# Two transformer blocks on one core: the same instructions, other SBUF addresses

## The chip, the core and the metric

The kernel runs on one core of a Trainium2 chip. The metric is the device time of one execution in microseconds (us), as the median of several runs. The profile comes from one further execution, taken by the hardware profiler; its engines are PE (TensorE, the matmuls), PEld (TensorE's weight loads, which run beside PE), DVE (VectorE), ACT (ScalarE), POOL (GpSimd) and SP (which issues most DMAs).

## What is computed

A network of two blocks of two layers each, for 256 tokens of `x` and 256 tokens of context, all in float32 with a model width of 1024. Cut to its skeleton:

```python
def first_block(x, c, ctx, ...):
    for i in range(2):
        sh1, sc1, ga1, sh2, sc2, ga2 = split(silu(c) @ w_ada[i] + b_ada[i], 6)
        hx = rms_norm(x, g_mix[i]) * (1 + sc1) + sh1
        zx = hx @ w_in[i]
        mx = concat([attention(q, k, v), pool_mix(...), fourier_mix(...)])
        x = x + ga1 * (mx @ w_out[i])
        fx = rms_norm(x, g_ffn[i]) * (1 + sc2) + sh2
        x = x + ga2 * swiglu(fx, w_gate_up[i], w_down[i])
        ...
def second_block(x, c, ctx, ...):
    for i in range(2):
        ...
        y = merge_branches(conv, differential_attention, gates)
        x = x + gx1 * y
        x = x + gx2 * (square(relu(h @ w1)) @ w2)
def reference(...):
    return second_block(first_block(x, ...), ...)
```

The context stream goes through the same steps, except in the last layer of each block. Most of the work is the product of 256 or 512 token columns with large weight matrices.

## The kernel before

**The product.** Activations lie in SBUF feature by feature: 128 features on the partitions, 256 or 512 tokens along each partition. So that a product in the fast `float32r` format keeps float32 accuracy, both operands are split into a high and a low half, and three products are summed in PSUM: high times high, high times low, low times high. Weights come in pieces of 512 rows by 256 columns: `load` (L89) issues one DMA into a `raw` tile of 128 x 1024, `wunits` (L97) makes the high half `wh` with a cast on ACT (L110) and the low half `wl` with a subtraction on DVE, or in some stages on POOL (L111). The pools `raw`, `whp` and `wlp` hold 3, 4 and 4 such tiles.

**Which operand moves.** In `proj` (L120) the weight slice is the stationary operand of 128 x 128 and the activation is the moving one, 512 or 256 columns wide. These are L142 (high, high), L143 (high, low) and L144 (low, high). L165 to L167 in `proj_split` and L528 to L530 in `proj_early` are the same with 256 columns. In `projt` (L170), which makes queries, keys, values and other token-major results, it is the other way round: the activation is stationary and the weight slice moves, 256 columns, in L184 to L186. `shift_product` (L487) has a stationary operand of only four columns per chunk, `sh[:, k, :]`, and moves the weight slices past it (L493). Two lines of `proj` and one of `shift_product`:

```python
nc.tensor.matmul(o, lhsT=hi[k][:, w], rhs=a, start=(k == order[0]), stop=False)   # L142
nc.tensor.matmul(o, lhsT=hi[k][:, w], rhs=b, start=False, stop=False)             # L143
nc.tensor.matmul(ps[:4, :256], lhsT=sh[:, k, :], rhs=w[k], ...)                   # L493
```

**Other places that the text speaks of.** Attention keeps its probabilities and their transposes in the pool `ap`: L663 writes an exponential into a fresh `ap` tile, L673 transposes it on PE, L867 copies the transpose into another, and L846 reads that in the product with the values. The convolution of the second block (`tap`, L1040) runs on DVE in L1060: for each of 31 taps it multiplies the input, shifted by d = -15 to 15 tokens, by a weight and adds it into an accumulator tile; with both streams its shape is 2 x (256 - |d|) elements, so 128x500 is a shift of 6 tokens, 24 bytes. The modulation vectors are made by `ada_load` and `ada_mul` (L311) from weights that are loaded straight into `act` tiles.

**What sets the order.** Source order, priorities (`soon`, `first`) and the tile scheduler. Each engine then works through its own list of instructions in order.

**Where the tiles lie.** Pools are placed one behind the other in the order in which `Net.__init__` makes them. In the built program (bytes per partition) the constants start at 16512 and hold some small tiles, then `raw` follows at 34016, `whp` at 46304, `wlp` at 62688, `act` at 89632. So every `raw`, `wh` and `wl` tile starts 96 bytes past a multiple of 128, and every tile of `act`, `tmp`, `ap`, `hd`, `zo` and `po` 32 bytes past one. Slices step by 512 or 1024 bytes and keep that remainder. Every float32r product thus has its moving and its stationary operand at the same place modulo 64 bytes, namely 32, save the 64 of L493.

Of the kernel before, what the change touches and what calls it, by code (L numbers as in the profile page):

```python
# [12 lines left out]
F32R = mybir.dt.float32r  # L13
# [5 lines left out]
P = 128  # L19
D = 1024  # L20
KC = 8
T = 256
EPS = 1e-6
NACT = 42
# [3 lines left out]
class Net:  # L28
    def __init__(self, ctx, tc, a, out):
        self.tc, self.nc, self.a, self.out = tc, tc.nc, a, out  # L30
        pool = lambda name, bufs, **k: ctx.enter_context(tc.tile_pool(name=name, bufs=bufs, **k))
        self.cp = pool("cp", 1)
        self.raw = pool("raw", 3)
        self.whp = pool("whp", 4)
        self.wlp = pool("wlp", 4)
        self.lay = pool("lay", 2)
        self.pools = {
            "act": (pool("act", NACT), 512),
            "tmp": (pool("tmp", 5), 512),
            "ap": (pool("ap", 11), 512),  # L40
            "hd": (pool("hd", 4), 512),
            "zo": (pool("zo", 3), 512),
            "po": (pool("po", 4), 256),
            "ti": (pool("ti", 6), 16),
            "tn": (pool("tn", 4), 16),
            "th": (pool("th", 8), 16),
            "ta": (pool("ta", 20), 16),
        }
        self.psum = {n: pool("ps" + n, b, space=PSUM) for n, b in
                     (("mm", 3), ("S", 2), ("T", 1), ("po", 1), ("ms", 1))}  # L50
        self.n = 0
        self.queue = []
        self.bg = []
        self.loaded, self.summed = [], []
        self.lo_count, self.lo_share = 0, 0
        self.depth = 2
        self.count, self.rate, self.held, self.gap = 0, 1, False, False
        self.units = []
        self.late = []
# [37 lines left out]
    def wunits(self, src):  # L97

        nc = self.nc
        kk = src.shape[0] // P  # L100
        hi, lo = [], []
        k = 0
        while k < kk:
            m = min(4, kk - k)
            with self.soon():
                raw = self.load(src[k * P : (k + m) * P, :])
                h = self.whp.tile([P, 1024], F32R, tag="wh", name=self.nm("wh"))
                l = self.wlp.tile([P, 1024], F32R, tag="wl", name=self.nm("wl"))
                r = raw[:, : m * 256]
                nc.scalar.copy(h[:, : m * 256], r)  # L110
                self.lo_engine().tensor_tensor(l[:, : m * 256], r, h[:, : m * 256].bitcast(F32), op=ALU.subtract)  # L111
            for i in range(m):
                hi.append(h[:, i * 256 : (i + 1) * 256])
                lo.append(l[:, i * 256 : (i + 1) * 256])
            k += m
        if not self.held:
            self.tick()
        return hi, lo
# [107 lines left out]

    def setup(self):
        nc = self.nc
        self.ident = self.const([P, P], "ident")
        make_identity(nc, self.ident)  # L230
        self.ones = self.const([P, 1], "ones")
        nc.vector.memset(self.ones, 1.0)
        self.lnw = self.const([P, P], "lnw")
        nc.vector.memset(self.lnw, 1.0 / 512)
        self.mhalf = self.const([P, 16], "mhalf")
        nc.vector.memset(self.mhalf, -0.5)
        self.xT = [self.const([P, 512], f"xT{k}") for k in range(KC)]
        self.cv = {}

    def cond(self, sfx):  # L240
# [1158 lines left out]
```

## Time and profile before

| | us |
|---|---|
| median of 3 runs (2423.03 to 2424.59) | 2423.99 |
| the profiled execution, its own time | 2417.76 |
| its span, first to last instruction | 2416.0 |
| PE busy | 2318.3 |
| PEld busy | 1964.4 |
| DVE busy | 1417.6 |
| ACT busy | 1024.3 |
| POOL busy | 437.1 |

The profiled execution took 6.2 us less than the median of the three timed runs, and 1.76 us more than its own span. The mean granted clock of TensorE was 0.982 of 2.4 GHz. A matmul's duration in the profile includes its way through the array and overlaps the next one's; how fast matmuls follow each other is read from the distance between two starts.

### The profile page before, as it was taken

What the parts mean: (1) busy time and instruction counts of PE and PEld (TensorE: products, weight loads), DVE (VectorE), ACT (ScalarE), POOL (GpSimd) and SP (SyncE); (2) the same over time, 40 slices, a digit from 0 to 9 for tenths busy, and PEclk for the clock granted to TensorE, in tenths of its full rate; (3) what the DMA queues carried; (4) which work ended last, traced back from release to release, by engine and by line L of the source; (5) the groups of instructions that cost most, each with busy time, mean ns of one, the idle gap of its engine ahead of it and who ended that gap; (6) DMA issues with size and microseconds to landing.
All of it is one profiled execution on the core that took longest, in us unless ns stands there. A gap on an engine that the chain in (4) does not pass through costs nothing.

```text
span 2416.0 us, 38908 instructions
## 1 busy us (share of the span) xinstructions
PE 2318.3 (96%) x15444; PEld 1964.4 (81%) x15444; DVE 1417.6 (59%) x2740; ACT 1024.3 (42%) x1786; POOL 437.1 (18%) x318
## 2 busy tenths in 40 slices
PE   6999999999989999997899999999999999999999
PEld 4867888888858999886675778888788887799999
DVE  5755643434665556489967436633333589947554
ACT  4544522222554445434546433623223544555543
POOL 2300000001110000356731200101101253330111
PEclk8999999999999999999899999999999999999999
DMA  8673443434583775322141223444345332155654
GB/s 261 185 249 123 130 141 114 140 105 153 165 258 123 249 243 160 120 88 70 64 129 45 74 84 102 125 140 152 119 139 180 106 99 71 62 158 166 192 178 145
DMA packets 338198, 338.65 MB, mean 140 GB/s; under 512 B 14692, under 2 KB 334912, under 8 KB 338016
## 3 DMA queue, kind: packets, MB, share of 16 engines
q1 hardware_dynamic: 336064, 334.81, 43.9%
q0 software_dynamic: 1952, 1.36, 0.4%
q8 instruction: 121, 1.98, 0.4%
q14 instruction: 61, 0.50, 0.1%
HBM read 335.06 MB, written 1.05 MB: 139 GB/s over the span
## 4 chain that ended last, share of the span: by engine, by line
PE 70%; DVE 14%; issue 8%; DMA 3%; ACT 2%; POOL 2%; SPq 0%; POOLq 0%; ACTq 0%; DVEq 0%
PE pmm L142 17%; PE pmm L144 17%; PE pmm L143 16%; DVE act L1060 5%; PE pms L311 3%; DMA act<-in_w_ada_dram 2%; PE pmm L184 2%; PE pmm L186 2%; PE pmm L185 2%; DVE wl L111 2%; PE pS L649 1%; PE pT L673 1%; DVE ta L658 1%; PE pmm L166 1%; PE pmm L167 1%
## 5 line engine op out<-in xcount | busy, mean ns | idle before, releaser
L142 PE MATMUL pmm<-act,wh 128*128 128x256 f32 (+1 forms) x2724 | 912.2, 337 | 8.3 <-ACT act L195 8.1
L143 PE MATMUL pmm<-act,wh 128*128 128x256 f32 (+1 forms) x2724 | 909.7, 334 | 1.2 <-DVE act L196 1.0
L144 PE MATMUL pmm<-act,wl 128*128 128x256 f32 (+1 forms) x2724 | 907.9, 335 | 0.0
L111 DVE TENSOR_TENSOR wl<-raw,wh 128x1024 fp32r<-128x1024 f32 x384 | 476.0, 1241 | 517.1 <-ACT wh L110 512.0
L110 ACT CAST wh<-raw 128x1024 fp32r<-128x1024 f32 x436 | 453.7, 1042 | 753.2 <-PE pmm L143 489.8
L142 PEld LDWEIGHTS pmm<-act,wh 128*128 128x128 f32 x2724 | 512.5, 189 | 69.7 <-ACT act L195 10.3
L144 PEld LDWEIGHTS pmm<-act,wl 128*128 128x128 f32 x2724 | 514.0, 189 | 58.5 <-issue 3.1
L143 PEld LDWEIGHTS pmm<-act,wh 128*128 128x128 f32 x2724 | 514.3, 189 | 57.4 <-DVE act L196 2.9
L184 PE MATMUL pmm<-wh,act 128*128 128x256 f32 x960 | 277.3, 289 | 4.6 <-ACT hd L582 3.6
L185 PE MATMUL pmm<-wl,act 128*128 128x256 f32 x960 | 275.0, 287 | 0.9 <-DVE wl L111 0.9
L186 PE MATMUL pmm<-wh,act 128*128 128x256 f32 x960 | 273.6, 286 | 1.3 <-DVE act L196 1.3
L184 PEld LDWEIGHTS pmm<-wh,act 128*128 128x128 f32 x960 | 185.8, 194 | 20.8 <-issue 11.8
L185 PEld LDWEIGHTS pmm<-wl,act 128*128 128x128 f32 x960 | 185.8, 194 | 11.3 <-issue 9.8
L186 PEld LDWEIGHTS pmm<-wh,act 128*128 128x128 f32 x960 | 185.4, 194 | 9.4 <-issue 7.6
L111 POOL TENSOR_TENSOR wl<-raw,wh 128x1024 fp32r<-128x1024 f32 x52 | 134.4, 2585 | 230.7 <-ACT wh L110 182.3
L1060 DVE SCALAR_TENSOR_TENSOR act<-act,wdw,act 128x486 f32<-128x486 f32 (+29 forms) x210 | 163.3, 795 | 0.5
L663 ACT ACTIVATE ap<-pS,ta 128x512 f32<-128x512 f32 (+1 forms) x144 | 88.9, 617 | 160.1 <-DVE ta L660 159.6
L196 DVE TENSOR_TENSOR act<-tmp,act 128x256 fp32r<-128x256 f32 (+1 forms) x193 | 101.8, 541 | 93.1 <-ACT act L195 92.6
L547 DVE SCALAR_TENSOR_TENSOR xT<-pmm,ada,xT 128x256 f32<-128x256 f32 x216 | 94.1, 478 | 77.2 <-PE pmm L144 71.1
L1216 POOL TENSOR_TENSOR tmp<-tmp 128x512 f32<-128x512 f32 x45 | 63.7, 1417 | 399.9 <-ACT tmp L1215 347.4
L195 ACT CAST act<-tmp 128x256 fp32r<-128x256 f32 (+1 forms) x193 | 90.0, 483 | 88.4 <-POOL tmp L1216 59.9
L223 POOL TENSOR_TENSOR tn<-tn,mhalf 128x2 f32<-128x2 f32 (+1 forms) x16 | 13.1, 817 | 600.5 <-DVE tn L221 592.8
(230 smaller groups left out, 2649.9 us busy)
## 6 DMA issues: line engine op xcount, KB each, us to landing
act<-in_w_ada_dram SPq DMA_DIRECT2D x384, 256.0 KB, 5.7
raw<-in_w_mlp_dram SPq DMA_DIRECT2D x128, 512.0 KB, 3.8
raw<-in_w_in_dram SPq DMA_DIRECT2D x116, 512.0 KB, 3.8
raw<-in_w_gate_up_dram SPq DMA_DIRECT2D x88, 512.0 KB, 3.6
raw<-in_w_down_dram SPq DMA_DIRECT2D x40, 512.0 KB, 4.4
raw<-in_w_out_dram SPq DMA_DIRECT2D x32, 512.0 KB, 3.8
raw<-in_w_attn_out_dram SPq DMA_DIRECT2D x16, 512.0 KB, 3.5
raw<-in_w_conv_out_dram SPq DMA_DIRECT2D x8, 512.0 KB, 3.6
```

Of the source, the lines that this page charges most:

```text
L110: nc.scalar.copy(h[:, : m * 256], r)
L111: self.lo_engine().tensor_tensor(l[:, : m * 256], r, h[:, : m * 256].bitcast(F32), op=ALU.subtract)
L142: nc.tensor.matmul(o, lhsT=hi[k][:, w], rhs=a, start=(k == order[0]), stop=False)
L143: nc.tensor.matmul(o, lhsT=hi[k][:, w], rhs=b, start=False, stop=False)
L144: nc.tensor.matmul(o, lhsT=lo[k][:, w], rhs=a, start=False, stop=(k == order[-1]))
L184: nc.tensor.matmul(o, lhsT=xh[k][:, t], rhs=hi[k], start=(k == 0), stop=False)
L185: nc.tensor.matmul(o, lhsT=xh[k][:, t], rhs=lo[k], start=False, stop=False)
L186: nc.tensor.matmul(o, lhsT=xl[k][:, t], rhs=hi[k], start=False, stop=(k == n - 1))
L195: self.nc.scalar.copy(hi, src)
L196: self.nc.vector.tensor_tensor(lo, src, hi.bitcast(F32), op=ALU.subtract)
L547: self.nc.vector.scalar_tensor_tensor(self.xT[k][:, c], ps[:, o : o + T], A[:, gb + k, q : q + 1], self.xT[k][:, c], op0=ALU.mult, op1=ALU ...
L1060: nc.vector.scalar_tensor_tensor(av[:, :, lo:hi], zv[:, :, lo + d : hi + d], wt, av[:, :, lo:hi], op0=ALU.mult, op1=ALU.add)
```

## The change

Three things in `Net.__init__`, `wunits` and `setup`. The pools of large tiles are made first (`raw`, `act`, `tmp`, `ap`, `hd`, `zo`, `po`, then `whp` and `wlp`), and the constants, the layer tiles and the pools of small tiles after them; among the constants the eight `xT` tiles come first. A `wh` or `wl` tile is 1040 instead of 1024 elements wide, and the 1024 that are used start at element 0, 4, 8 or 12: for `wh` by the running number of the weight piece modulo 4, for `wl` by that number divided by 4, modulo 4. And `ap` has 10 buffers instead of 11.

```diff
-        self.cp = pool("cp", 1)
         self.raw = pool("raw", 3)
+        sizes = {"act": (NACT, 512), "tmp": (5, 512), "ap": (10, 512), "hd": (4, 512), "zo": (3, 512), "po": (4, 256)}
+        self.pools = {n: (pool(n, b), w) for n, (b, w) in sizes.items()}
         self.whp = pool("whp", 4)
         self.wlp = pool("wlp", 4)
+        self.cp = pool("cp", 1)
         self.lay = pool("lay", 2)
-        self.pools = {
-            "act": (pool("act", NACT), 512),
-            "tmp": (pool("tmp", 5), 512),
-            "ap": (pool("ap", 11), 512),
...
-        }
+        self.pools |= {n: (pool(n, b), 16) for n, b in (("ti", 6), ("tn", 4), ("th", 8), ("ta", 20))}
...
-        self.n = 0
+        self.n = self.wn = 0
...
-                h = self.whp.tile([P, 1024], F32R, tag="wh", name=self.nm("wh"))
-                l = self.wlp.tile([P, 1024], F32R, tag="wl", name=self.nm("wl"))
+                a, b = 4 * (self.wn % 4), 4 * (self.wn // 4 % 4)
+                self.wn += 1
+                h = self.whp.tile([P, 1040], F32R, tag="wh", name=self.nm("wh"))[:, a : a + 1024]
+                l = self.wlp.tile([P, 1040], F32R, tag="wl", name=self.nm("wl"))[:, b : b + 1024]
...
+        self.xT = [self.const([P, 512], f"xT{k}") for k in range(KC)]
         self.ident = self.const([P, P], "ident")
...
-        self.xT = [self.const([P, 512], f"xT{k}") for k in range(KC)]
```

In the built program `raw` now starts at 16512, `act` at 28800, `ap` at 125056, `whp` at 163968 and `wlp` at 180608. Tiles of `raw`, `act`, `tmp`, `ap`, `hd`, `zo`, `po` and `xT` start at a multiple of 128. A buffer of `whp` or `wlp` is 4160 bytes, so their starts alternate between 0 and 64 past a multiple of 128; with the offset added, a half starts at 0, 16, 32 or 48 modulo 64. The instructions of all five engines stand in the same order as before, tile for tile; only instructions that do nothing but wait differ in number (three fewer on ACT, one more on DVE).

## Rows read from the trace of the kernel before

**Rows 1.** The page, busy time: engine, us, share of the span, instructions
```profile
PE 2318.3 (96%) x15444; PEld 1964.4 (81%) x15444; DVE 1417.6 (59%) x2740; ACT 1024.3 (42%) x1786; POOL 437.1 (18%) x318
```
**Rows 2.** The page, shares of the chain that ended last, by engine and line
```profile
PE 70%; DVE 14%; issue 8%; DMA 3%; ACT 2%; POOL 2%; SPq 0%; POOLq 0%; ACTq 0%; DVEq 0%
PE pmm L142 17%; PE pmm L144 17%; PE pmm L143 16%; DVE act L1060 5%; PE pms L311 3%; DMA act<-in_w_ada_dram 2%; PE pmm L184 2%; PE pmm L186 2%; PE pmm L185 2%; DVE wl L111 2%; PE pS L649 1%; PE pT L673 1%; DVE ta L658 1%; PE pmm L166 1%; PE pmm L167 1%
```
**Rows 3.** Groups by line and shape, PE: xcount | busy us, mean ns
```profile
L142 PE MATMUL pmm<-act,wh 128*128 128x512 f32 x1300 | 512.7, 397 | 2.6 <-ACT act L195 2.5
...
L142 PE MATMUL pmm<-act,wh 128*128 128x256 f32 x1424 | 399.5, 283 | 5.7 <-ACT act L195 5.5
...
L184 PE MATMUL pmm<-wh,act 128*128 128x256 f32 x960 | 277.3, 289 | 4.6 <-ACT hd L582 3.6 <-ACT act L195 1.0
...
L166 PE MATMUL pmm<-act,wh 128*128 128x256 f32 x248 | 69.4, 281 | 0.3 <-DVE act L196 0.3
...
L529 PE MATMUL pmm<-act,wh 128*128 128x256 f32 x96 | 27.2, 283 | 0.0
```
**Rows 4.** Groups, ACT: the cast that makes the high halves, and its idle time
```profile
L110 ACT CAST wh<-raw 128x1024 fp32r<-128x1024 f32 x428 | 448.7, 1050 | 743.3 <-PE pmm L143 486.3 <-issue 107.6 <-PE pmm L186 61.3
```
**Rows 5.** Stretch of 160 to 630 us: busy (instructions), granted clock, DMA
```profile
160.00:630.00 470.00, 465.96 (x2524) 374.67 (x2523) 214.54 (x406) 148.80 (x243) 9.13 (x16) 1.00 0.43 135
```
**Rows 6.** Timeline of PE, 512 columns in `proj`: start us, us, instruction
```profile
457.21 0.39 PE L144 MATMUL pmm<-act,wl 128*128 128x512 f32 x1
457.44 0.39 PE L142 MATMUL pmm<-act,wh 128*128 128x512 f32 x1
457.68 0.39 PE L143 MATMUL pmm<-act,wh 128*128 128x512 f32 x1
457.90 0.39 PE L144 MATMUL pmm<-act,wl 128*128 128x512 f32 x1
...
459.05 0.39 PE L143 MATMUL pmm<-act,wh 128*128 128x512 f32 x1
```
**Rows 7.** Timeline of PE, 256 columns, activation moving, at 2216 us
```profile
2216.10 0.28 PE L528 MATMUL pmm<-act,wh 128*128 128x256 f32 x1
...
2217.04 0.28 PE L530 MATMUL pmm<-act,wl 128*128 128x256 f32 x1
```
**Rows 8.** The same, 256 columns, activation moving, at 915 us
```profile
914.74 0.28 PE L144 MATMUL pmm<-act,wl 128*128 128x256 f32 x1
...
916.10 0.28 PE L144 MATMUL pmm<-act,wl 128*128 128x256 f32 x1
```
**Rows 9.** Timeline of PEld at 2216 us: a weight load
```profile
2216.34 0.19 PEld L528 LDWEIGHTS pmm<-act,wh 128*128 128x128 f32 x1
```
**Rows 10.** Timeline of PE, L493, four stationary columns, two passes
```profile
766.62 0.28 PE L493 MATMUL pms<-wl,po 128*4 128x256 f32 x1
...
767.53 0.28 PE L493 MATMUL pms<-wl,po 128*4 128x256 f32 x1
...
2218.22 0.28 PE L493 MATMUL pms<-wl,po 128*4 128x256 f32 x1
...
2219.03 0.28 PE L493 MATMUL pms<-wh,po 128*4 128x256 f32 x1
```
**Rows 11.** Timeline of DVE, convolution taps of 6 and 3 tokens' shift
```profile
1065.42 0.72 DVE L1060 SCALAR_TENSOR_TENSOR act<-act,wdw,act 128x500 f32<-128x500 f32 x1
...
1071.58 0.73 DVE L1060 SCALAR_TENSOR_TENSOR act<-act,wdw,act 128x506 f32<-128x506 f32 x1
```
**Rows 12.** Timeline in the first layer's attention: two users of one `ap` buffer
```profile
121.72 0.76 PE L673 MATMUL pT<-ident,ap 128*128 128x128 f32 x4
...
125.14 0.47 ACT L663 ACTIVATE ap<-pS,ta 128x256 f32<-128x256 f32 x1
```
**Rows 13.** Waits of PE: us in total, times, longest us
```profile
PE pmm L311 <- DMA act<-in_w_ada_dram: 7.3, 5, 3.2
...
PE pmm L185 <- DVE wl L111: 0.9, 1, 0.9
```

More of the change, by code (lines that the diff above doesn't have):

```diff
@@ L31, in __init__ @@
         pool = lambda name, bufs, **k: ctx.enter_context(tc.tile_pool(name=name, bufs=bufs, **k))
-        self.cp = pool("cp", 1)
         self.raw = pool("raw", 3)
+        sizes = {"act": (NACT, 512), "tmp": (5, 512), "ap": (10, 512), "hd": (4, 512), "zo": (3, 512), "po": (4, 256)}
+        self.pools = {n: (pool(n, b), w) for n, (b, w) in sizes.items()}
         self.whp = pool("whp", 4)
         self.wlp = pool("wlp", 4)
+        self.cp = pool("cp", 1)
         self.lay = pool("lay", 2)
-        self.pools = {
-            "act": (pool("act", NACT), 512),
-            "tmp": (pool("tmp", 5), 512),
-            "ap": (pool("ap", 11), 512),
[L41 to L47, printed above, removed]
-        }
+        self.pools |= {n: (pool(n, b), 16) for n, b in (("ti", 6), ("tn", 4), ("th", 8), ("ta", 20))}
         self.psum = {n: pool("ps" + n, b, space=PSUM) for n, b in
                      (("mm", 3), ("S", 2), ("T", 1), ("po", 1), ("ms", 1))}
-        self.n = 0
+        self.n = self.wn = 0
         self.queue = []
```

## The prediction

> **What bounds the kernel now.** I read the page's busy times first: PE is busy for 96% of the span, DVE, the next of the computing engines, for 59% [rows 1]. The chain that ended last says the same: 70% of it lies on PE, and the six lines of the weight products (L142 to L144, L184 to L186) hold 17, 16, 17, 2, 2 and 2%, 56% together [rows 2]. The weights are not late: ACT's cast, the first step of a weight half, sat idle 743.3 us in front of its 428 large instructions, and most of that ended with a matmul that gave a buffer back (486.3 us behind L143, 61.3 us behind L186) [rows 4]. PE in turn lost 7.3 us to the loads of the modulation weights and 0.9 us to DVE's low halves in L185 [rows 13]. So the time is set by how fast float32r matmuls follow each other. How many there are is in the groups by shape: three lines of 1300 with 512 columns, 3900; three each of 1424, 248 and 96 with 256 columns and a moving activation, 5304; three of 960 with a moving weight, 2880 [rows 3].
>
> How fast they follow each other stands in the timeline. With 512 columns, eight starts take from 457.21 to 459.05 us, 230 ns each [rows 6]. With 256 columns, at 2216 us, eight take from 2216.10 to 2217.04, 117.5 ns each [rows 7]; at 915 us the same kind of instruction, twelve from 914.74 to 916.10, takes 113.3 ns [rows 8]. The granted clock of the stretch from 160 to 630 us is 1.00, the upper level of 2.4 GHz [rows 5], at which 512 columns pass in 213 ns and 256 in 107 ns. So there are 17 ns above the columns in a 512-column step and 6.6 or 10.8 ns in a 256-column step, and rows 7 and 8 hold two levels for one shape.
>
> **The change, part by part.** It moves no instruction on any engine; the program differs in addresses, in one buffer, and in four instructions that only wait. The arithmetic, the tiles' contents and the DMAs' sizes stay.
>
> *One `ap` buffer fewer.* A tile in `ap` must wait until the last reader of the tile that had its buffer is done. I laid the buffers that the built change assigns over the times of the trace: of its 234 re-uses the closest is a tile that L663 starts to write at 125.14 us in a buffer that L673 last read in the group that ended at 121.72 + 0.76 = 122.48 us [rows 12]. That leaves 2.66 us, so no instruction would wait: **0 us**. The cover is that distance. If it were gone, ACT would stand in L663, with the copies L867 behind it, and PE in the next transposes; even three such places of 2.7 us would cost 8 us, the far end. Below nothing there is no gain, since a buffer taken away frees nobody.
>
> *Writes and reads of DVE, ACT and POOL at other addresses.* The convolution taps already read their input at any multiple of 4 bytes from where they accumulate: a shift of 6 tokens is 24 bytes and one of 3 tokens is 12, and neither lies on a multiple of 16. They take 0.72 us for 500 elements and 0.73 us for 506 [rows 11], the same per element. So DVE's low halves, which are now written 16, 32 or 48 bytes further, cost **0 us** more. ACT and POOL have no such row; ACT's idle time in front of the casts covers a change there of some per cent.
>
> *Loads into other addresses.* PE waits for loads in 7.3 us [rows 13]. A gain is at most that; a load that took longer would first eat into ACT's idle time. **0 us**.
>
> *TensorE's reads.* This is the disputed term. Before, the moving and the stationary operand of every large product start at 32 modulo 64 bytes. After, a moving activation starts at 0, and the stationary or moving weight half at 0, 16, 32 and 48 in nearly equal shares. No row shows a float32r product with a moving start at 0 modulo 64, or a full-width stationary operand at another place modulo 64 than the moving one, so the cost has to be bounded. The far end of a gain is that all time above the columns goes: 17 ns x 3900 + 10.8 ns x 5304 = 66 + 57 = 123 us. Towards a loss the nearest rows are the two levels: if the 2880 products with a moving weight and the 3900 wide ones rose by the ratio of the levels, 117.5 / 113.3 = 1.037, that is 4.2 ns x 2880 + 8.5 ns x 3900 = 12 + 33 = 45 us.
>
> I take **0 us**, for three reasons. The level changes while the addresses do not: rows 7 and 8 have the same starts modulo 512 and differ by 4.2 ns. With 512 columns the step behind L142 is 0.24 us and the one behind L143 is 0.22 us [rows 6], again with the same starts; what differs is which half is read. And L493 is the one place that already walks through the relations: its stationary operand moves on by 16 bytes with each chunk, past weights that stay at 96. From 766.62 to 767.53 us, eight steps, it passes all four relations modulo 64 at 114 ns each; from 2218.22 to 2219.03, seven steps, it passes them again at 116 ns [rows 10]. The level belongs to the pass, not to the relation. L493 loads only four columns, so this bears on the starts and not on a long weight read; but it is the nearest row.
>
> A weight load takes 0.19 us [rows 9] in a step of 117.5 ns, so a load is in flight beside every product and the two reads do overlap; read that way the extra time could be theirs. The Trainium skill, page "SBUF — State Buffer", section "Who interferes with whom", gives TensorE two independent read ports, one for the moving operand and one for the weight load, and lets it wait for nobody; by that rule the offsets of the halves are worth 0 us, while by the overlap read as a conflict they could be worth up to the 123 us above. No run so far decides between them for a full weight load.
>
> *Sum.* 0 + 0 + 0 + 0. The profiled execution would take 2417.8 us again. The runs' median lies 6.2 us above it, and measured against that I say **2424 us**. Small shifts can let a stretch fall to the other level: 350 steps of 256 columns, some 40 us, change by 350 x 4.2 ns = 1.5 us, so I give this case 2420 to 2428 on its own.
>
> **The rivals.**
>
> *A. The start of the moving operand sets the level.* An activation that starts at 0 instead of 32 modulo 64 would need fewer accesses, and products with a moving activation would go to the lower level. For it: the time above the columns is there in every row and nobody else causes it, and the 256-column products fall on two sharp levels. Against it: rows 7 and 8. The price: 4.2 ns x 5304 = 22 us, and the same 3.6% on 512 columns, 8.3 ns x 3900 = 32 us; 54 us in all, 2370 us. Some stretches are at the lower level already and PE also waits elsewhere, so about half of it is the likelier result: some 2397 us. The Trainium skill, page "TensorE: Matmul & The Clock Gate", section "Back-to-back issue gap", states N / 2.4 + 2.5 ns for a product at the full clock, 109 and 216 ns; an estimate by that page puts the products' gain at (117.5 - 109) x 5304 + (230 - 216) x 3900, about 100 us, and this trace disagrees with the page so far, at 117.5 and 230 ns [rows 6, 7].
>
> *B. The relation between the two reads matters, and 0 was the good one.* Slower than before: the relation was 0 modulo 64 everywhere and becomes 16, 32 or 48 for three quarters of the products. If those rise by a level, the 2880 with a moving weight and the 3900 wide ones pay 3/4 x 45 = 34 us: 2458 us; with one or two of the three relations bad, 2435 to 2447. It decides as soon as products with unequal relations follow each other more slowly than those with equal ones. For it: the overlap of loads and products. Against it: L493 passes the four relations without a step.
>
> *C. The alignment is not what the words say.* In part this is certain: a weight buffer of 4160 bytes puts every second one at 64 modulo 128, so the starts modulo 128 are 0, 80, 32 and 112 for `wh`. If only 128 counted, the mixture would be another one, and the result is inside A or B.
>
> **How the numbers follow.** The forecast has 0.47, A 0.31, B 0.22; C has no chance of its own. What a measurement of this kernel can tell from no change is about 0.2%, 4.8 us. The forecast falls inside that nearly always; A and B nearly never. That gives faster 0.33, same 0.45, slower 0.22. The range from 2388 to 2442 holds the forecast, the likelier half of A (about 0.20 of its 0.31) and three quarters of B, some 0.83 together; what is left out is A at its full price and B with all three relations bad. The far ends of the unknown, 123 us of gain and 45 us of loss, lie outside it.
>
> **What would show it.** If the forecast is right, the timeline of the change has 256-column steps at 113 and 117.5 ns and 512-column steps at 230 ns as before, for weight pieces with any offset, the busy time of PE stays within 5 us of 2318, and L663 has no new wait in the first layer's attention. A shows itself by 256-column steps at 113 ns or below nearly everywhere and wide ones below 226, alike for all pieces. B shows itself by steps whose length changes from one weight piece to the next, in a pattern of four. A wait of ACT for PE before L663 or L867 would prove the `ap` term wrong. I am wrong as a whole if PE's busy time moves by more than 10 us.

## The result and the profile after

The change made the kernel slower. Its median is 2447.69 us (2444.30 to 2450.99, four runs) against 2424.03 us before (2423.03 to 2424.59, four runs), a ratio of 1.0098 with a 95% interval of 1.0080 to 1.0115. The profiled execution took 2444.30 us, with a span of 2442.5 us: 26.5 us more than before. The forecast was 2424 us; the upper end of the range, 2442 us, was missed by 5.7 us. The time went the way of rival B.

The page after, busy times:

```profile
PE 2349.5 (96%) x15444; PEld 1981.3 (81%) x15444; DVE 1415.9 (58%) x2740; ACT 1024.9 (42%) x1786; POOL 441.0 (18%) x318
```

The chain after that ended last, by engine and by line (line numbers behind `wunits` are lower by 7, so L142 to L144 are now L135 to L137, and L184 to L186 are L177 to L179):

```profile
PE 73%; DVE 13%; issue 8%; DMA 3%; ACT 2%; POOL 1%; SPq 0%; POOLq 0%; DVEq 0%; ACTq 0%
PE pmm L135 17%; PE pmm L136 17%; PE pmm L137 16%; DVE act L1053 5%; PE pms L304 3%; PE pmm L177 3%; PE pmm L179 3%; PE pmm L178 3%; DMA act<-in_w_ada_dram 2%; PE pS L642 2%; DVE wl L104 2%; PE pT L666 1%; PE ppo L1296 1%; PE pmm L159 1%; PE pmm L160 1%
```

PE's busy time went from 2318.3 us [rows 1] to 2349.5, or 31 us more for the same 15444 matmuls, and that of its weight loads (PEld) rose with it, from 1964.4 us to 1981.3. DVE, ACT and POOL are within 4 us. The share of PE in the chain went from 70% [rows 2] to 73%. The groups after, by line and shape, with the idle time in front of them at the end of each row:

```profile
L135 PE MATMUL pmm<-act,wh 128*128 128x512 f32 x1300 | 514.9, 398 | 2.6 <-ACT act L188 2.5
...
L103 ACT CAST wh<-raw 128x1024 fp32r<-128x1024 f32 x428 | 448.1, 1048 | 758.9 <-PE pmm L136 506.7 <-issue 105.0 <-PE pmm L179 65.0
...
L135 PE MATMUL pmm<-act,wh 128*128 128x256 f32 x1424 | 401.4, 285 | 5.5 <-ACT act L188 5.5
...
L177 PE MATMUL pmm<-wh,act 128*128 128x256 f32 x960 | 280.6, 293 | 4.7 <-ACT hd L575 3.6 <-ACT act L188 1.0
...
L159 PE MATMUL pmm<-act,wh 128*128 128x256 f32 x248 | 69.9, 283 | 0.3 <-DVE act L189 0.3
...
L522 PE MATMUL pmm<-act,wh 128*128 128x256 f32 x96 | 27.5, 286 | 0.0
```

Every group of weight products is up by 1 to 4 ns a product [rows 3], and PE does not wait longer for what it reads: the idle time in front of L135 and L177 is that of before, and the cast, which had 743.3 us of idle time [rows 4], now has 758.9, most of it still behind matmuls. Weights arrive earlier than PE wants them, as before. PE's wait for the loads of the modulation weights, 7.3 us before [rows 13], did not grow either (in total, times, longest):

```profile
PE pmm L304 <- DMA act<-in_w_ada_dram: 6.4, 5, 2.9
```

Where it shows is the timeline. These are the first of the three products (L135) in one stretch with 512 columns after; the columns are start, duration, engine, line and instruction:

```profile
514.83 0.39 PE L135 MATMUL pmm<-act,wh 128*128 128x512 f32 x1
515.51 0.39 PE L135 MATMUL pmm<-act,wh 128*128 128x512 f32 x1
516.19 0.39 PE L135 MATMUL pmm<-act,wh 128*128 128x512 f32 x1
...
518.23 0.40 PE L135 MATMUL pmm<-act,wh 128*128 128x512 f32 x1
518.93 0.40 PE L135 MATMUL pmm<-act,wh 128*128 128x512 f32 x1
519.63 0.40 PE L135 MATMUL pmm<-act,wh 128*128 128x512 f32 x1
520.34 0.40 PE L135 MATMUL pmm<-act,wh 128*128 128x512 f32 x1
...
523.87 0.39 PE L135 MATMUL pmm<-act,wh 128*128 128x512 f32 x1
```

A piece of weights serves eight such triples of products. Up to 518.23 us both halves of the piece have offset 0, and a triple takes 3.40 / 5 = 0.680 us. Then comes the next piece, whose high half has offset 16 and lies in another of the four buffers: by the built program it starts 208 bytes behind the moving read and the low half 192 bytes behind it, modulo 256. From 518.93 to 523.87, seven triples, each takes 0.706 us. Sixteen pieces earlier, at 421 us, where both halves had offset 0 the time before, the triples reached 680 ns too, and the piece behind it went to 706 or 707. So the pace follows the piece, as B said it would, though with a delay: the first three triples of the piece with offset 0, from 512.75 us on, still took 693, 695 and 690 ns.

**Where the 26 us are.** I took the distance between the starts of successive triples in every stretch where nothing held PE up (triples up to 720 ns for 512 columns and 375 ns for 256, some nine in ten of those of `proj`). Their mean went from 686.8 to 697.8 ns for 512 columns (1300 triples: +14.3 us), from 352.0 to 355.5 ns in `proj` with 256 (1424: +5.0 us), and from 343.9 to 354.7 ns in `projt` (960: +10.4 us). Comparing the start of the same PE instruction in both traces gives the same picture by stage: the two wide stages, 160 to 624 and 1300 to 1893 us, lost 5.8 and 9.4 us; the stages that are mostly narrow, 700 to 1240 us and 2060 us to the end, 3.1 and 2.2. Of the `projt` products most lie in stages where PE also waits for attention and convolution, so not all of their loss need reach the end. Two short stages added 4.5 and 3.1 us, and the stages left over gave 1.6 us back. In the two short ones PE was granted a lower clock than before: the trace has the lower level, 1.2 GHz, from 1275.6 to 1285.9 us, after PE had sat idle 0.73, 0.44 and 0.28 us between short attention products, and from 2053.9 to 2060.7 us, after an idle time of 2.44 us. The two windows of before and the two of after hold the same work; the columns are the window and its length, busy time (instructions) of PE, PEld, DVE, ACT and POOL, granted clock, DMA share and GB/s. Before:

```profile
1242.00:1294.00 52.00, 48.63 (x305) 32.65 (x303) 30.94 (x106) 26.10 (x68) 5.76 (x5) 1.00 0.29 92
2011.00:2057.00 46.00, 43.24 (x306) 35.90 (x306) 45.90 (x103) 21.58 (x43) 20.45 (x11) 1.00 0.23 69
```

After:

```profile
1249.00:1306.00 57.00, 53.68 (x310) 36.31 (x308) 31.11 (x107) 26.61 (x69) 5.78 (x5) 0.91 0.27 85
2032.00:2081.00 49.00, 46.56 (x307) 38.32 (x306) 46.90 (x104) 21.89 (x43) 20.29 (x11) 0.93 0.21 65
```

These two are not tied to one layout: by the same comparison the runs below have from 0.0 to 13.9 us in the first and from -0.1 to 3.0 in the second. Why the clock fell there in one run and not in another was not settled. So 20.5 of the 26.5 us lie in the stages that the weight products fill, and 7.6 us in the two where the clock was lower.

### The profile page after: what moved, and what is told of

Its sections match the earlier page's. It is cut to its first block, busy times and chain, and to the rows that moved or that the text cites. A ratio compares the mean times of both kernels' runs of the same rounds, so it can differ in the third digit from the quotient of the medians.

```text
span 2442.5 us, 38906 instructions
## 1 busy us (share of the span) xinstructions
PE 2349.5 (96%) x15444; PEld 1981.3 (81%) x15444; DVE 1415.9 (58%) x2740; ACT 1024.9 (42%) x1786; POOL 441.0 (18%) x318
## 4 chain that ended last, share of the span: by engine, by line
PE 73%; DVE 13%; issue 8%; DMA 3%; ACT 2%; POOL 1%; SPq 0%; POOLq 0%; DVEq 0%; ACTq 0%
PE pmm L135 17%; PE pmm L136 17%; PE pmm L137 16%; DVE act L1053 5%; PE pms L304 3%; PE pmm L177 3%; PE pmm L179 3%; PE pmm L178 3%; DMA act<-in_w_ada_dram 2%; PE pS L642 2%; DVE wl L104 2%; PE pT L666 1%; PE ppo L1296 1%; PE pmm L159 1%; PE pmm L160 1%
## 5 line engine op out<-in xcount | busy, mean ns | idle before, releaser
L135 PE MATMUL pmm<-act,wh 128*128 128x256 f32 (+1 forms) x2724 | 916.4, 339 | 8.1 <-ACT act L188 8.0
L137 PE MATMUL pmm<-act,wl 128*128 128x256 f32 (+1 forms) x2724 | 912.8, 336 | 0.0
L104 DVE TENSOR_TENSOR wl<-raw,wh 128x1024 fp32r<-128x1024 f32 x384 | 475.8, 1240 | 529.3 <-ACT wh L103 528.3
L103 ACT CAST wh<-raw 128x1024 fp32r<-128x1024 f32 x436 | 453.0, 1040 | 768.4 <-PE pmm L136 512.4
L135 PEld LDWEIGHTS pmm<-act,wh 128*128 128x128 f32 x2724 | 513.5, 189 | 76.3 <-ACT act L188 10.0
L137 PEld LDWEIGHTS pmm<-act,wl 128*128 128x128 f32 x2724 | 514.5, 189 | 61.3 <-issue 3.1
L177 PE MATMUL pmm<-wh,act 128*128 128x256 f32 x960 | 280.6, 293 | 4.7 <-ACT hd L575 3.6
L179 PE MATMUL pmm<-wh,act 128*128 128x256 f32 x960 | 276.3, 289 | 1.3 <-DVE act L189 1.3
L177 PEld LDWEIGHTS pmm<-wh,act 128*128 128x128 f32 x960 | 186.0, 194 | 21.2 <-issue 12.2
L179 PEld LDWEIGHTS pmm<-wh,act 128*128 128x128 f32 x960 | 185.9, 194 | 9.4 <-issue 7.6
L656 ACT ACTIVATE ap<-pS,ta 128x512 f32<-128x512 f32 (+1 forms) x144 | 89.1, 619 | 155.3 <-DVE ta L653 154.8
```

The costliest lines, as they stand in the source:

```text
L137: nc.tensor.matmul(o, lhsT=lo[k][:, w], rhs=a, start=False, stop=(k == order[-1]))
L177: nc.tensor.matmul(o, lhsT=xh[k][:, t], rhs=hi[k], start=(k == 0), stop=False)
L179: nc.tensor.matmul(o, lhsT=xl[k][:, t], rhs=hi[k], start=False, stop=(k == n - 1))
```

## The experiments

The theories at the start: **R**, the relation of the two reads modulo 64 bytes sets the pace (rival B); **M**, the start of the activation does (rival A); **S**, it is the switch from one offset to the next that breaks a rhythm; **W**, the missing `ap` buffer makes waits. Later came **A** (not rival A; it concerns the start of both reads), **D**, **Q** and **L**, which the expectations define. Below, a triple is three products of one chunk, as above, and *d* is the start of the stationary read minus that of the moving read, modulo 256 bytes. Read off the built programs, *d* was 192 before in products with a moving activation and 64 in `projt`, where weights move.

| run | d (bytes) | 512 columns, ns per triple | 256, activation moves (`proj`) | 256, weight moves | PE busy, us |
|---|---|---|---|---|---|
| before | 192; `projt` 64 | 686.8 | 352.0 | 343.9 | 2318.3 |
| after | mixed | 697.8 | 355.5 | 354.7 | 2349.5 |
| e1_align_only | 0 | 681.1 | 359.8 | 359.1 | 2336.9 |
| e2_offsets_only | mixed | 697.4 | 354.5 | 354.0 | 2349.6 |
| e3_ap10_only | 192; `projt` 64 | 686.8 | 349.0 | 343.7 | 2317.0 |
| e4_constant_16 | 16 past 0, 64, 128, 192 | 697.6 | 355.2 | 353.9 | 2349.9 |
| e5_diff64 | 64 and 192 in turn | 695.1 | 341.9 | 350.6 | 2326.8 |
| e6_start32 | 0 | 681.1 | 359.7 | 359.0 | 2338.6 |
| e7_constant_32 | 32 past 0, 64, 128, 192 | 700.2 | 354.5 | 354.4 | 2359.9 |
| e8_by_stage | 512: 0; 256: 64 | 681.1 | 341.6 | 347.5 | 2293.5 |
| e9_diff128 | 128 | 697.8 | 356.1 | 356.2 | 2360.1 |
| e10_by_stage_192 | 512: 0; 256: 192 | 681.1 | 352.8 | 351.9 | 2321.3 |

The fourth column is `proj` alone, 1424 of the 1768 narrow triples with a moving activation. The 248 of `proj_split` went 350.3 ns before, 359.6 in run 1, 342.1 in run 5, 350.0 in run 8 and 352.4 in run 10; the 96 of `proj_early` 351.4, 359.4, 345.6, 347.4 and 351.3. Run 3 has the distance of before and 349.0 ns against 352.0, so a mean at one distance is not fixed to better than some 3 ns. PE busy holds the stretches of lower clock too: 13.9 and 8.9 us of runs 7 and 9 lie in the first of the two windows above, and the triples are the fairer comparison.

Ratios are to the kernel before on the same chip; the number of timed runs is in brackets.

**The change taken apart, 1: the alignment alone.** The new order of the pools and 10 `ap` buffers, but halves of 1024 elements without an offset:

```diff
-                h = self.whp.tile([P, 1040], F32R, tag="wh", name=self.nm("wh"))[:, a : a + 1024]
-                l = self.wlp.tile([P, 1040], F32R, tag="wl", name=self.nm("wl"))[:, b : b + 1024]
+                h = self.whp.tile([P, 1024], F32R, tag="wh", name=self.nm("wh"))
+                l = self.wlp.tile([P, 1024], F32R, tag="wl", name=self.nm("wl"))
```

> The change without the offsets: the large pools first, ap with 10 buffers, every wh and wl half 1024 wide and at 0 modulo 128, so that the moving and the stationary operand of every large product start at 0. Theory R (the relation of the two starts modulo 64 sets the pace, and equal starts are the good case): back to 2424 us, from 2415 to 2430; 512-column triples (three products of one chunk) at 680 to 687 ns as in the profile of before, not 698. Theory M (the activation's start at 0 instead of 32 costs): stays at 2440 to 2455. Theory S (it is the switch of relation from one weight piece to the next that breaks a settled rhythm, whatever the relation): 2424 us. Theory W (the missing ap buffer makes ACT wait): 2440 to 2455.

Measured: 2430.61 us (11), ratio 1.0039 (1.0025 to 1.0053). A little slower: the wide triples gained 6 ns and the narrow ones lost 8 to 15. Wide and narrow first products in its timeline:

```profile
345.40 0.39 PE L133 MATMUL pmm<-act,wh 128*128 128x512 f32 x1
...
352.20 0.39 PE L133 MATMUL pmm<-act,wh 128*128 128x512 f32 x1
...
2164.83 0.28 PE L133 MATMUL pmm<-act,wh 128*128 128x256 f32 x1
...
2168.79 0.28 PE L133 MATMUL pmm<-act,wh 128*128 128x256 f32 x1
```

Ten triples in 6.80 us are 680 ns; eleven in 3.96 us are 360 ns. Before, the narrow ones at this place took 2164.80 to 2168.68, eleven in 3.88, that is 353 ns:

```profile
2164.80 0.28 PE L142 MATMUL pmm<-act,wh 128*128 128x256 f32 x1
...
2168.68 0.28 PE L142 MATMUL pmm<-act,wh 128*128 128x256 f32 x1
```

**2: the offsets alone.** The kernel before, with its pools in their old order, with halves of 1040 and the rotating offsets, and 10 `ap` buffers, which make the room:

```diff
-            "ap": (pool("ap", 11), 512),
+            "ap": (pool("ap", 10), 512),
...
+                a, b = 4 * (self.wn % 4), 4 * (self.wn // 4 % 4)
+                self.wn += 1
+                h = self.whp.tile([P, 1040], F32R, tag="wh", name=self.nm("wh"))[:, a : a + 1024]
+                l = self.wlp.tile([P, 1040], F32R, tag="wl", name=self.nm("wl"))[:, b : b + 1024]
```

> The layout of before with the rotating offsets alone (and ap with 10 buffers, since the wider halves would not fit otherwise): activations start at 32 modulo 64, halves at 32 plus 0, 16, 32 or 48. Theories R and S: 2440 to 2455 us, as with the whole change. Theory M: 2424 us. Theory W: 2440 to 2455.

Measured: 2440.79 us (5), 1.0083 (1.0069 to 1.0097). Without the new order of the pools, the offsets with their wider slots are worth nearly the whole loss. The activations still start at 32, so M falls.

**3: the `ap` buffer alone.**

```diff
-            "ap": (pool("ap", 11), 512),
+            "ap": (pool("ap", 10), 512),
```

> The kernel before with 10 instead of 11 ap buffers, nothing else but the 2048 bytes by which the pools behind it move up. Theories R, S and M: 2424 us, within 3 us. Theory W: 2440 us or more, with ACT waiting for PE in the softmax.

Measured: 2419.92 us (11), 0.9986 (0.9972 to 1.0000). W falls: the buffer costs nothing.

**4: no rotation.** The changed kernel with the same offset, 16 bytes, for every half:

```diff
-                a, b = 4 * (self.wn % 4), 4 * (self.wn // 4 % 4)
+                a, b = 4, 4
```

> The change with the same offset of 16 bytes for every half: the relation of the two starts is 16 modulo 64 everywhere and never switches. Theory S: 2424 us, one settled rhythm. Theory R: slower than 2424; by the triples with both halves at 16 in the profile of the change (700 ns against 687 with 512 columns, 351 as before with 256) about 17 us on the wide products and 5 to 10 us on those with a moving weight, 2440 to 2455. Theory M: 2440 to 2455.

Measured: 2443.71 us (4), 1.0087 (1.0074 to 1.0100). As slow as the rotation, though the offset never changes. Slots of 4160 bytes still move *d* by 64 bytes from piece to piece, so by itself this run excludes a switch modulo 64 alone. But between two triples of one piece nothing switches, and there the wide triples took 696 to 699 ns at each of *d* = 16, 80, 144 and 208. Run 9, where *d* is one and the same throughout, is as slow too. So S falls: it is the standing distance that costs, not the switch.

**5: 64 bytes instead of 0.** That the alignment alone, with both reads equal modulo 64 bytes as before, moved the wide triples one way and the narrow ones the other fits neither R nor M as a whole. Two things had changed together: where the reads start (32 before, 0 then, modulo 64) and their distance modulo 128 (64 before, 0 then). This run keeps the start and restores the distance:

```diff
-                h = self.whp.tile([P, 1024], F32R, tag="wh", name=self.nm("wh"))
+                h = self.whp.tile([P, 1056], F32R, tag="wh", name=self.nm("wh"))[:, 16:1040]
```

(the same for `wl`; compared with the alignment alone)

> The halves, all at one place, are moved by 64 bytes: activations start at 0 of every 128 bytes, the weights' halves at 64, so that the two reads of a product stand 0 apart of 64, as before and in the run with the alignment alone, but 64 apart of 128 (there 0). Theory A (where a product's reads start, of 64 bytes, sets the pace of the small products: 0 is the slow start, 32 the fast one, the distance of 128 does not count): as with the alignment alone, three products 256 wide 360 ns and 512 wide 681 ns, PE busy 2337 us, ratio to before 1.003 to 1.005. Theory D (the distance of 128 bytes counts, and 64 was the good one of before): 256 wide 340 to 353 ns, 512 wide 687 ns, PE busy 2317 to 2323 us, ratio 0.998 to 1.001.

Measured: 2419.96 us (12), 1.0002 (0.9987 to 1.0017). The narrow triples went from 360 to 342 ns, so the distance counts, as D said; here eleven in 3.74 us, 340 ns each:

```profile
2164.98 0.28 PE L133 MATMUL pmm<-act,wh 128*128 128x256 f32 x1
...
2168.72 0.28 PE L133 MATMUL pmm<-act,wh 128*128 128x256 f32 x1
```

The wide ones missed what D gave: 695 ns, not 687. A buffer of 1056 elements is 4224 bytes, so its halves stand 64 and 192 bytes behind the activation in turn, and the wide triples differ by just that: 699 ns at 64 (582 triples), 691 at 192 (555). The modulus is thus at least 256. That 256 is enough shows in run 8 below: there the narrow triples of `proj` stand 64 or 320 bytes apart modulo 512, and took 341.5 and 341.8 ns.

**6: another start, the same distance.** The alignment alone behind a tile of 32 bytes, so that all reads start at 32 modulo 64 as before, and *d* is 0:

```diff
+        self.pad = pool("pad", 1).tile([P, 8], F32, tag="pad", name="pad")
         self.raw = pool("raw", 3)
```

> The alignment alone behind one tile of 32 bytes: activations and halves all start at 32 of every 128 bytes, 0 apart. Theory A (start of 64 bytes counts): as before, 256 wide 340 to 353 ns a triple, 512 wide 687 ns, PE busy 2317 to 2323 us, ratio 0.998 to 1.001. Theory D (the distance of 128 counts, the start does not): as the alignment alone, 360 and 681 ns, PE busy 2337 us, ratio 1.003 to 1.005.

Measured: 2432.12 us (11), 1.0049 (1.0033 to 1.0066), and the triples are those of the alignment alone to 0.1 ns. Where the two reads start makes no difference while their distance is kept; A falls, and M once more.

**7: 32 bytes apart.** The changed kernel with

```diff
-                a, b = 4 * (self.wn % 4), 4 * (self.wn // 4 % 4)
+                a, b = 8, 8
```

> The changed kernel with both halves always 32 bytes behind the aligned place: activations at 0, weights at 32 of 64. Theory R (any two reads that stand unequal of 64 bytes are slow): as with the constant 16, 512 wide 697 ns, 256 wide 354 to 355 ns, PE busy 2350 us, ratio 1.007 to 1.010. Theory R16 (only 16 and 48 are bad, 32 apart is as good as 0): 512 wide 681 to 687 ns, PE busy 2317 to 2337 us, ratio 0.998 to 1.005.

Measured: 2439.62 us (6), 1.0094 (1.0066 to 1.0122). R holds here: 32 apart is no better than 16. In all runs where the distances are no multiple of 64, the wide triples average 697 to 700 ns and the narrow ones 354 to 356, in many different lengths. Piece by piece the narrow ones spread: 350 ns at *d* = 208 (run 4), 352 at 224 and 353 at 96 (run 7), but 358 at 144 and 160. So for the wide shape every such distance was slow; for the narrow one 208 and 224 were no slower than the 352 ns of before.

**8, 9, 10: the distance chosen by stage.** Slots of 1088 elements, 17 x 256 bytes, put every half at the same place modulo 256, and an argument says where it starts: 0 or 16 elements behind that place in `proj`, 16 in `proj_split` and `proj_early`, 48 in `projt`, where weights move. The rest is the alignment alone. Run 8:

```diff
-    def wunits(self, src):
+    def wunits(self, src, o=0):
...
+                h = self.whp.tile([P, 1088], F32R, tag="wh", name=self.nm("wh"))[:, o : o + 1024]
...
-        hi, lo = self.wunits(src)
+        hi, lo = self.wunits(src, 0 if nT == 512 else 16)
...
-        ws = [self.wunits(src) for src, _ in jobs]
+        ws = [self.wunits(src, 16) for src, _ in jobs]
...
-        hi, lo = self.wunits(src)
+        hi, lo = self.wunits(src, 48)
```

> The alignment alone with slots of 1088 columns, so that every half starts at the same place of 256 bytes, and a start chosen by stage: the stationary read starts 0 bytes behind the moving one (of 256) in the products 512 wide, 64 bytes behind it in those 256 wide, with the weights on either side. Theory Q (the distance of the two reads modulo 256 sets the pace, wherever they start; read off the runs so far): a triple 512 wide 681 ns, 256 wide 341 to 342 ns with stationary weights and 344 to 348 ns with moving ones, ratio to before 0.990 to 0.995. Theory L (the rhythm is what the stretch happened to lock into; the run with 64 bytes had both 64 and 192 in turn): 256 wide 350 to 360 ns, ratio 0.998 to 1.004.

Measured: **2398.65 us** (6), 0.9911 (0.9895 to 0.9927): faster than both kernels. Its busy times:

```profile
PE 2293.5 (96%) x15444; PEld 1948.2 (81%) x15444; DVE 1416.9 (59%) x2740; ACT 1024.7 (43%) x1786; POOL 439.7 (18%) x318
```

The first products of a wide and a narrow stretch in its timeline:

```profile
345.09 0.39 PE L133 MATMUL pmm<-act,wh 128*128 128x512 f32 x1
...
351.89 0.39 PE L133 MATMUL pmm<-act,wh 128*128 128x512 f32 x1
...
2149.88 0.28 PE L133 MATMUL pmm<-act,wh 128*128 128x256 f32 x1
...
2153.62 0.28 PE L133 MATMUL pmm<-act,wh 128*128 128x256 f32 x1
```

Ten wide triples in 6.80 us, 680 ns; eleven narrow ones in 3.74 us, 340 ns. PE is busy 24.8 us less than before and 56 us less than with the change, with the same instructions in the same order.

Run 9 has `o=32`, 128 bytes, in all products:

> As the one before, but the stationary read starts 128 bytes behind the moving one, of 256, in all products. Theory Q, if 128 counts: a pace of its own, neither 681 and 360 ns (distance 0) nor 687 and 340 to 353 ns (64 and 192). If only 128 bytes counted, as theory D said: 681 and 360 ns as with distance 0, ratio 1.003 to 1.005.

Measured: 2443.88 us (6), 1.0094 (1.0077 to 1.0110). 128 is a distance of its own, and a bad one; ten wide triples take 6.97 us, 697 ns each:

```profile
345.27 0.39 PE L133 MATMUL pmm<-act,wh 128*128 128x512 f32 x1
...
352.24 0.39 PE L133 MATMUL pmm<-act,wh 128*128 128x512 f32 x1
```

With *d* = 128 the two reads stand equal modulo 64 bytes, so R is wrong in its modulus.

Run 10 exchanges 16 and 48 in run 8:

> As the run by stage, but 192 bytes in place of 64 for the products 256 wide. Theory Q: 512 wide 681 ns; 256 wide as in the rows where the distance was 192: 352 ns with stationary weights (kernel before), 353 ns with moving ones; ratio 0.997 to 1.002, so some 10 us slower than with 64. Theory L: no difference from the run with 64.

Measured: 2414.02 us (10), 0.9973 (0.9959 to 0.9987), 15 us more than with 64. The same stretch as above with its pace of 353 ns, eleven in 3.88 us:

```profile
2164.74 0.28 PE L133 MATMUL pmm<-act,wh 128*128 128x256 f32 x1
...
2168.62 0.28 PE L133 MATMUL pmm<-act,wh 128*128 128x256 f32 x1
```

Theory Q gave both times, and the paces of `proj` and `projt` within some ns; L gave neither time. But `proj_split` in run 8 took 350.0 ns, not the 341 to 342 that Q had for stationary weights: it stands where L put it. And something else goes beyond Q: at 192 the narrow triples with a moving activation take 349 to 353 ns when all pieces stand there (before, runs 3 and 10), and 342 when pieces at 64 and 192 alternate (run 5). So the distance sets the pace in the mean of `proj`, and something more decides which of two rhythms, 340 or 353 ns, a narrow stretch takes. It may keep the rhythm that it came in with; that was not tried by itself. That `projt` took 343.9 ns before and 347.5 in run 8 at the same distance is open too.

## Why the prediction was wrong

**The bound** was right: the pace of the float32r products set the time, and PE's busy time moved by 31 us while nothing waited longer for weights.

**The `ap` buffer, the loads, and the addresses of DVE, ACT and POOL** at 0 us were right as far as runs show: run 3 for the buffer, and DVE's 1417.6 us became 1415.9. L656, which was to start 2.66 us after its buffer came free [rows 12], shows no wait for PE.

**The term that failed is "TensorE's reads: I take 0 us".** The profiled executions differ by 26.5 us, and 20.5 us of that lie in the stages that the weight products fill; the 7.6 us of the two stages with the lower clock are in no term of the sum. The prediction counted the relation of the two reads modulo 64 bytes, by which all products were alike before. Modulo 256 they were not: *d* was 192 in `proj` and 64 in `projt`. Its three reasons fell one by one.
- *"The level changes while the addresses do not"* [rows 7, 8]. True, and no evidence: one distance showed more than one rhythm. Before, 134 of 1283 steady narrow triples took 340 ns and 1140 took 353 or 354; at *d* = 64 (run 8) the count is 1118 at 340. The distance shifts how often each rhythm comes, and two levels at one address say nothing against that.
- *"What differs is which half is read"* [rows 6]. The step of 0.24 us is not behind L142 by nature. At another place of the kernel before, it stands behind L144:

```profile
1700.30 0.39 PE L144 MATMUL pmm<-act,wl 128*128 128x512 f32 x1
1700.54 0.39 PE L142 MATMUL pmm<-act,wh 128*128 128x512 f32 x1
1700.77 0.39 PE L143 MATMUL pmm<-act,wh 128*128 128x512 f32 x1
1700.99 0.39 PE L144 MATMUL pmm<-act,wl 128*128 128x512 f32 x1
```

  0.24, 0.23 and 0.22 us, in a rhythm of three. Most often the longest of the three steps stands behind L142, but in well over a hundred steady triples each behind L143 and behind L144. With *d* = 0 all three steps are 226 to 228 ns.
- *"L493 walks through the relations without a step"* [rows 10]. It loads four columns, not 128; the prediction said so, and gave it the weight of the nearest row all the same. In every run its steps average 115 or 116 ns, whatever the layout did to the full-width products, so it could tell nothing about them. The rows that carried the disputed read, a full load of 0.19 us in flight beside every product [rows 9], were in the text.

**Rival B** was right that the relation of the two reads matters, and in its side. It was wrong in which relations are good, and mis-sized. "0 was the good one", modulo 64, does not hold: at *d* = 128 the reads are equal modulo 64 and the kernel is as slow as with the change (run 9, 1.0094), and at *d* = 0 the narrow triples are at their slowest, 360 ns. As to its size: spread over all pieces, three quarters of its steps, it had 3.2 ns for products with a moving weight, 6.4 ns for wide ones and none for the 5304 narrow ones with a moving activation. Measured were 10.8 / 3 = 3.6, 11.0 / 3 = 3.7 and 3.5 / 3 = 1.2 ns. That the 2447.69 us lie beside the 2447 that B gave for two bad relations is luck: 16 and 32 are bad by runs 4 and 7, in the rotation the wide pieces with both offsets at 48 took 700 ns as well, and part of the loss came with the clock.

**Rival A** fell with run 6. Its gain on wide products is there (687 to 681 ns, run 1), but from the distance, not from the start, and what it promised for narrow products came out as a loss of 8 ns a triple.

**The rule on the read ports.** Runs 1 and 5 differ in nothing but where the halves lie, and the narrow triples in 360 against 342 ns. The Trainium skill, page "SBUF — State Buffer", section "Who interferes with whom", lets the moving read and the weight load go by two independent ports that wait for nobody, so that the place of the halves would cost nothing; this case's traces disagree with that for full-width float32r products. That the two reads hold each other up is the nearest reading, but no run here shows the reads themselves, and why the distance counts stays open. The Trainium skill, page "TensorE: Matmul & The Clock Gate", section "Back-to-back issue gap", gives 109 and 216 ns by its formula, which it states for an isolated product. This case's traces lie above both: the best paces of these runs are 340 / 3 = 113.3 and 680 / 3 = 226.7 ns.

## What to carry to other kernels

Where a kernel is bound by back-to-back float32r matmuls, the place of the stationary tile relative to the moving one is a parameter to measure, by shape: of the distances tried here 0 modulo 256 bytes was best for 512 columns and 64, in most stretches, for 256 columns, while 128 was bad for both and anything that is no multiple of 64 bad for 512. Aligning every tile alike, or spreading them over offsets, is no safe choice; read the distance between starts over several steps in the timeline. And where the only row against a rival is of another shape than the disputed instruction, its chance belongs higher than that row alone would have it.

## What was not expected of the hardware

- The commonest lengths of the steady triples are sharp: 340, 353 and 360 ns at *d* = 64, 192 and 0, and 680 and 687 ns at 0 and 192, with 700 frequent at the other distances, where the wide ones scatter. These are whole multiples of 6.67 ns (51, 53, 54 and 102, 103, 105), the time of 16 cycles at 2.4 GHz. By the prediction's reckoning of one column a cycle that is 16 columns, or 64 bytes of a float32 row, and a triple takes 3, 5 or 6 such units more than its 48, and 6, 7 or 9 more than its 96.
- The two shapes want opposite things. At *d* = 0 the wide triple is at its best (681 ns) and the narrow one at its worst (360); at *d* = 64 it is 699 and 342.
- At *d* = 0, moving both reads by 32 bytes (runs 1 and 6) left every mean within 0.1 ns; their distance modulo 256 is what counted.
